# Normalizing one head of each retention pair on ScalarE instead of VectorE, in a two-layer streaming encoder

## The chip, the cores and the metric

One core of one Trainium2 chip runs the whole program. The metric is the device time of one execution in microseconds; lower is better. A core has five engines that run their own instruction streams in order and wait for each other through semaphores: TensorE (PE, with its weight loads as PEld), VectorE (DVE), ScalarE (ACT), GpSimd (POOL) and SyncE (SP), whose queue starts the DMA transfers. L12 in a profile line is line 12 of the kernel.

## What is computed

A sequence of 1024 tokens with 1024 channels passes through two layers. The first holds a state-space mixer and, beside it, a retention with 8 heads. Only the end of the retention is touched here:

```python
out = (intra_out + cross).reshape(bsz, seq, RET_HEADS, RET_DV)     # 8 heads of 128
mu = jnp.mean(out, axis=-1, keepdims=True)
var = jnp.mean(jnp.square(out - mu), axis=-1, keepdims=True)
out = (out - mu) * lax.rsqrt(var + EPS)
...
y_ret = retention(q, k, v).astype(h.dtype) * jax.nn.silu(g_ret)
```

Each token's 128 values of a head are centred and divided by their spread. The result is multiplied by a gate and goes, with the state-space branch, through an output projection; then come the convolution layer and a last norm.

## The kernel before

Nearly all large products are written as three TensorE matmuls of a high and a low part of each operand (lines L277, L278, L279), so TensorE has work through the whole program. The other engines prepare operands: a weight tile `wf` is loaded by DMA, ScalarE casts it to its high part `wh`, and VectorE or GpSimd makes the low part `wl`.

The retention runs over four pairs of heads (`ret_heads`, once for each pair). Within a pair the 1024 tokens are two halves `hf` of four blocks `b4` of 128 tokens; `hh` is the head within the pair. For one half and one head:

- TensorE makes the 128x512 result `ro` in PSUM, one 128x128 block for each `b4`.
- VectorE takes statistics of each block (`st` at L1246, `mv` with mean and variance at L1247).
- ScalarE takes the square root into `rs` (L563), VectorE the reciprocal in place (L564).
- VectorE writes `on` = (block - mean) * `rs`, four instructions (L1252).
- TensorE transposes `on` into `rt` (L1260), and VectorE multiplies `rt` with the gate into `grl` (L1263).

Both heads' transposes of the first half stand on TensorE ahead of both heads' of the second half, with the head `hh` = 1 first each time, in one fixed chain of order. The tile `on` has three buffers, so the fourth `on` of a pair (second half, `hh` = 1) takes the buffer of the pair's first one and can be written only after that one's transposes.

Around this, TensorE works on the gated linear unit of the state-space branch (`mm_glu`), 24 matmuls for a block and half. ScalarE applies a tanh to each result in place (L1094, or L1325 in the later blocks) and VectorE multiplies it into `yg` (L1095), which SyncE stores. A further background chain, `weight_low`, loads half weight tiles `lf`, casts them on ScalarE into `lh` (L233), makes the low part on GpSimd or VectorE (L234) and stores it, for the second layer. After the transposes of a pair come the next pair's `ktp` transposes, VectorE's `kt` (L1170), and TensorE's `kv` products (L1187), which need `kt`.

A scheduler sets the order of each engine's instructions when the program is built, by priorities and its own estimate of times. The engines then keep that order, so an instruction that waits holds up everything behind it on its engine. Square roots and tanh need different tables on ScalarE; ACT_TABLE_LOAD rows mark a change of table.

Of the kernel before, what the change touches and what calls it, by code (L numbers as in the profile page):

```python
# [11 lines left out]
F32 = mybir.dt.float32  # L12
F32R = mybir.dt.float32r
I32 = mybir.dt.int32
AF = mybir.ActivationFunctionType
ALU = mybir.AluOpType
# [3 lines left out]
P = 128  # L20
# [39 lines left out]
class Trunk:  # L60
# [1098 lines left out]
    def ret_heads(self, pair, K, Q, qadds, V, turned):  # L1159
        nc, rp = self.nc, self.rp  # L1160
        v = nc.vector

        kt = rp.tile([P, 8, P], F32, name=f"kt_{pair}", tag="kt", bufs=1)
        for hf in range(2):
            ps = self.bank(f"ktp{hf}_{pair}")
            for b in range(4):
                t0 = (4 * hf + b) * P
                nc.tensor.transpose(ps[:, b * P:(b + 1) * P], K[:, t0:t0 + P], self.ident[:])
            kd = self.kdec[:, 2 * pair:2 * pair + 2, :].rearrange("p h d -> p (h d)")
            self.last_kt = v.tensor_tensor(kt[:, 4 * hf:4 * hf + 4, :], ps[:].rearrange("p (b d) -> p b d", b=4),  # L1170
                                           kd.unsqueeze(1).broadcast_to([P, 4, P]), op=ALU.mult)

        with self.tc.issue_after(self.last_kt.ins):
            for add in qadds:
                add()
        turned()

        S = rp.tile([P, 8, P], F32, name=f"S_{pair}", tag="S", bufs=1)
        for hf in range(2):
            ps = self.bank(f"kv{hf}_{pair}")  # L1180
            for b4 in range(4):
                b = 4 * hf + b4
                if b == 7:
                    continue
                for hh in range(2):
                    r = slice(64 * hh, 64 * hh + 64)
                    nc.tensor.matmul(ps[r, b4 * P:(b4 + 1) * P], kt[:, b, r], V(pair, b, hh),  # L1187
                                     start=True, stop=True)
            for b4 in range(4):
                b = 4 * hf + b4  # L1190
                if b == 7:
                    continue
                kv = ps[:, b4 * P:(b4 + 1) * P]
                if b == 0:
                    v.tensor_copy(S[:, 1, :], kv)
                else:
                    v.scalar_tensor_tensor(S[:, b + 1, :], S[:, b, :], self.g128[:, pair:pair + 1], kv,
                                           op0=ALU.mult, op1=ALU.add)

        self.masked = [None, None]  # L1200
        sc = [rp.tile([P, 8, P], F32, name=f"sc{hh}_{pair}", tag=f"sc{hh}", bufs=1) for hh in range(2)]
        for hf in range(2):
            sps = [self.bank(f"sp{hf}{hh}_{pair}") for hh in range(2)]
            self.chained(nc.tensor.matmul(sps[hh][:, b4 * P:(b4 + 1) * P],
                                          K[64 * hh:64 * hh + 64, (4 * hf + b4) * P:(4 * hf + b4 + 1) * P],
                                          Q[64 * hh:64 * hh + 64, (4 * hf + b4) * P:(4 * hf + b4 + 1) * P],
                                          start=True, stop=True)
                         for b4 in range(4) for hh in range(2))
            for hh in range(2):
                self.masked[hf] = v.tensor_tensor(  # L1210
                    sc[hh][:, 4 * hf:4 * hf + 4, :], sps[hh][:].rearrange("p (b i) -> p b i", b=4),
                    self.mask[:, 2 * pair + hh, :].unsqueeze(1).broadcast_to([P, 4, P]), op=ALU.mult)


        gts = []
        for hh in range(2):
            h = 2 * pair + hh
            gt = rp.tile([P, T], F32, name=f"grl_{h}", tag="grl", bufs=3)
            with self.tc.issue_after(self.masked[0].ins):
                nc.sync.dma_start(gt[:], self.gr_d[h * P:(h + 1) * P])  # L1220
            gts.append(gt)
        todo = []
        for hf in range(2):
            pss = [self.bank(f"ro{hf}_{2 * pair + hh}") for hh in range(2)]

            def products():
                for b4 in range(4):
                    b = 4 * hf + b4
                    for hh in range(2):
                        r = slice(64 * hh, 64 * hh + 64)  # L1230
                        if b:
                            yield nc.tensor.matmul(pss[hh][:, b4 * P:(b4 + 1) * P], Q[r, b * P:(b + 1) * P],
                                                   S[r, b, :], start=b4 == (hf == 0), stop=False)
                for hh in range(2):
                    for b4 in range(4):
                        b = 4 * hf + b4
                        yield nc.tensor.matmul(pss[hh][:, b4 * P:(b4 + 1) * P], sc[hh][:, b, :],
                                               V(pair, b, hh), start=False, stop=b4 == 3)
            last_ro = self.chained(products())
            ons = []  # L1240
            for hh in range(2):
                h, ps = 2 * pair + hh, pss[hh]
                st6 = rp.tile([P, 4, 6], F32, name=f"st_{h}_{hf}", tag="bst", bufs=2)
                mv = rp.tile([P, 4, 2], F32, name=f"mv_{h}_{hf}", tag="bmv", bufs=2)
                for b4 in range(4):
                    v.bn_stats(st6[:, b4, :], ps[:, b4 * P:(b4 + 1) * P])  # L1246
                    v.bn_aggr(mv[:, b4, :], st6[:, b4, :])  # L1247
                rs = rp.tile([P, 4], F32, name=f"rs_{h}_{hf}", tag="brs", bufs=2)
                self.last_rs = self.rsqrt(rs[:], mv[:, :, 1], eps=self.reps[:, h:h + 1])
                on = rp.tile([P, 4, P], F32, name=f"on_{h}_{hf}", tag="on", bufs=3)  # L1250
                for b4 in range(4):
                    v.tensor_scalar(on[:, b4, :], ps[:, b4 * P:(b4 + 1) * P], mv[:, b4, 0:1],  # L1252
                                                   rs[:, b4:b4 + 1], op0=ALU.subtract, op1=ALU.mult)
                ons.append(on)
            todo.append(ons)

            for hb in ((), (0, 1))[hf]:
                for hh in (1, 0):
                    tp = self.bank(f"rt{hb}_{2 * pair + hh}")
                    last_ro = self.chained((nc.tensor.transpose(tp[:, b4 * P:(b4 + 1) * P], todo[hb][hh][:, b4, :],  # L1260
                                                                self.ident[:]) for b4 in (3, 2, 1, 0)), last_ro)
                    c = slice(hb * HALF, (hb + 1) * HALF)
                    v.tensor_tensor(gts[hh][:, c], tp[:], gts[hh][:, c], op=ALU.mult)  # L1263
        for hh in range(2):
            h = 2 * pair + hh
            nc.sync.dma_start(self.yr_d[h * P:(h + 1) * P], gts[hh][:])
# [579 lines left out]
```

## Time and profile before

| | |
|---|---|
| time, 3 runs | 1177.71, 1180.71 (median), 1185.98 us |
| profiled execution, its own time | 1179.18 us |
| profiled execution, span of the trace | 1177.4 us |
| busy: PE, DVE, ACT, POOL | 1155.9, 954.2, 566.6, 718.3 us |
| granted TensorE clock, mean | 0.997 |
| retention pairs in the trace | about 517 to 635 us |

The span is what the instruction trace covers; the profiled execution's own time is 1.8 us longer. A timeline row gives the start, the length, the engine, the line, the operation with its output and inputs, how many equal instructions were merged, and in brackets how long the engine had been idle and what ended the wait. A window row gives for each engine the busy time and number of instructions in a stretch, and then the TensorE clock, the busy share of the DMA engines and their rate.

### The profile page before, as it was taken

Reading aid. Unit: us, or ns where it says so; the run is one execution under the profiler, and the core shown is the slowest. Engines: PE = TensorE matmul, PEld = TensorE weight load, DVE = VectorE, ACT = ScalarE, POOL = GpSimd, SP = SyncE. Lnnn points to the kernel's source line nnn. Section 1 sums busy time; section 2 is a strip of 40 time slices with the busy share of each in tenths; the row PEclk is TensorE's granted clock in tenths of the full one; section 3 lists DMA queues with packets and bytes.
Section 4 is the critical chain, followed back from the end, with each engine's and each line's share of the span. In section 5 each row is a group of like instructions: output and inputs, shape, how many; then the busy total and the mean of one; then the engine's idle time right before and its main releaser. Section 6 shows DMA issues by size and latency. Waiting matters only on the chain.

```text
span 1177.4 us, 17601 instructions
## 1 busy us (share of the span) xinstructions
PE 1155.9 (98%) x6102; PEld 958.2 (81%) x6102; DVE 954.2 (81%) x1541; ACT 566.6 (48%) x855; POOL 718.3 (61%) x499
## 2 busy tenths in 40 slices
PE   9999999999999999998999999999999999999997
PEld 7888788788887888877888788888888888888877
DVE  6889989999725666676888999579999999999643
ACT  7212342332236756413224846467756578544662
POOL 2049999888841143686532053439894689977742
PEclk9999999999999999999999999999999999999999
DMA  9359579877799979997676879975448653366863
GB/s 342 109 166 326 193 271 320 269 272 273 249 308 334 366 249 313 361 300 255 209 237 238 308 249 305 344 255 187 161 161 297 221 181 133 126 192 232 277 250 139
DMA packets 142137, 293.74 MB, mean 249 GB/s; under 512 B 14048, under 2 KB 42976, under 8 KB 141920
## 3 DMA queue, kind: packets, MB, share of 16 engines
q1 hardware_dynamic: 140896, 288.43, 72.2%
q10 hardware_dynamic: 1152, 4.19, 0.9%
q8 instruction: 48, 0.79, 0.3%
q14 instruction: 41, 0.34, 0.1%
HBM read 210.32 MB, written 81.20 MB: 248 GB/s over the span
## 4 chain that ended last, share of the span: by engine, by line
PE 70%; DVE 12%; DMA 10%; issue 3%; ACT 2%; SPq 1%; POOL 1%; DVEq 0%; ACTq 0%; POOLq 0%
PE mm_g L279 5%; PE mm_g L278 5%; PE mm_g L277 5%; PE mm_w L279 4%; PE mm_w L278 4%; PE mm_w L277 4%; PE mm_k L1026 4%; PE mm_a L279 2%; PE mm_b L278 2%; PE mm_a L278 2%; PE mm_b L279 2%; PE mm_a L277 2%; PE mm_b L277 2%; PE mm_oc L279 2%; PE mm_oc L278 2%
## 5 line engine op out<-in xcount | busy, mean ns | idle before, releaser
L1533 DVE SCALAR_TENSOR_TENSOR cv<-u,convw,cv 128x512 f32<-128x512 f32 x358 | 244.5, 748 | 4.5 <-ACT cv L1519 3.0
L1513 POOL TENSOR_TENSOR tp<-tp,tp 128x512 f32<-128x512 f32 x104 | 138.9, 1338 | 28.8 <-ACT tp L1512 23.5
L279 PE MATMUL mm_g<-xh,wl_g 128*128 128x512 f32 x256 | 100.8, 394 | 0.0
L278 PE MATMUL mm_g<-xl,wh_g 128*128 128x512 f32 x256 | 100.6, 393 | 0.0
L277 PE MATMUL mm_g<-xh,wh_g 128*128 128x512 f32 x256 | 100.4, 392 | 0.0
L1512 ACT ACTIVATE tp<-u,convw 128x512 f32<-128x512 f32 x104 | 69.8, 714 | 11.3 <-POOL tp L1513 11.0
L167 POOL TENSOR_TENSOR wl_K<-wf_K,wh_K 128x1024 fp32r<-128x1024 f32 x14 | 34.0, 2430 | 48.6 <-ACT wh_K L166 46.6
L278 PEld LDWEIGHTS mm_g<-xl,wh_g 128*128 128x128 f32 x256 | 48.1, 188 | 11.3 <-issue 1.6
L279 PEld LDWEIGHTS mm_g<-xh,wl_g 128*128 128x128 f32 x256 | 48.0, 188 | 10.5
L277 PEld LDWEIGHTS mm_g<-xh,wh_g 128*128 128x128 f32 x256 | 48.1, 188 | 9.6
L279 PE MATMUL mm_oc<-zh,wl_woc 128*128 128x512 f32 (+1 forms) x152 | 54.4, 359 | 0.6 <-DMA wl_woc<-lo_woc 0.6
L277 PE MATMUL mm_oc<-zh,wh_woc 128*128 128x512 f32 (+1 forms) x152 | 54.3, 361 | 0.0
L278 PE MATMUL mm_oc<-zl,wh_woc 128*128 128x512 f32 (+1 forms) x152 | 54.0, 356 | 0.0
L277 PE MATMUL mm_glu<-yh,wh_glu 128*128 128x512 f32 x128 | 51.2, 400 | 2.2 <-ACT yh L1270 2.2
L278 PE MATMUL mm_u<-xl,wh_u 128*128 128x512 f32 x128 | 50.0, 391 | 1.0 <-DVE xl L399 1.0
L278 PE MATMUL mm_glu<-yl,wh_glu 128*128 128x512 f32 x128 | 50.5, 394 | 0.2 <-DVE yl L1272 0.2
L279 PE MATMUL mm_glu<-yh,wl_glu 128*128 128x512 f32 x128 | 50.6, 396 | 0.0
L277 PE MATMUL mm_g<-h1h,wh_cg 128*128 128x512 f32 x128 | 50.3, 393 | 0.0
L277 PE MATMUL mm_a<-h1h,wh_ca 128*128 128x512 f32 x128 | 50.2, 392 | 0.0
L279 PE MATMUL mm_b<-h1h,wl_cb 128*128 128x512 f32 x128 | 50.2, 392 | 0.0
L279 PE MATMUL mm_a<-h1h,wl_ca 128*128 128x512 f32 x128 | 50.0, 390 | 0.0
L279 PE MATMUL mm_g<-h1h,wl_cg 128*128 128x512 f32 x128 | 49.8, 389 | 0.0
(834 smaller groups left out, 3671.9 us busy)
## 6 DMA issues: line engine op xcount, KB each, us to landing
wf_g<-w_ab SPq DMA_DIRECT2D x16, 512.0 KB, 6.2
a<-w_out SPq DMA_DIRECT2D x32, 256.0 KB, 4.5
ws<-a SPq DMA_DIRECT2D x32, 256.0 KB, 4.5
lf<-w_c SPq DMA_DIRECT2D x32, 256.0 KB, 5.1
wf_p<-ws SPq DMA_DIRECT2D x16, 512.0 KB, 4.8
wf_cb<-w_c SPq DMA_DIRECT2D x16, 512.0 KB, 5.0
wf_ca<-w_c SPq DMA_DIRECT2D x16, 512.0 KB, 4.8
wl_cb<-lo_cb SPq DMA_DIRECT2D x16, 512.0 KB, 3.3
```

What stands on the lines that cost most here:

```text
L167: e.tensor_tensor(wl[:].rearrange(fl), wf[:], wh[:].rearrange(fl).bitcast(F32), op=ALU.subtract)
L277: nc.tensor.matmul(ps, wh[:, kb, :], xh, start=start, stop=False, skip_group_check=chain)
L278: nc.tensor.matmul(ps, wh[:, kb, :], xl, start=False, stop=False, skip_group_check=chain)
L279: self.last_mm = nc.tensor.matmul(ps, wl[:, kb, :], xh, start=False, stop=stop, skip_group_check=chain)
L1026: self.last_mm = self.nc.tensor.matmul(ps, l[:, k, :], r[:], start=start and k == m == 0, stop=stop and k == 3 and m == 2, skip_group_chec ...
L1512: nc.scalar.mul(sk[:], u[:, k:k + HALF], cw[:, nb, k:k + 1])
L1513: gp.tensor_tensor(s0[:], s0[:], sk[:], op=ALU.add)
L1533: v.scalar_tensor_tensor(dst[:], *tap, accs_[i][:], op0=ALU.mult, op1=ALU.add)
```

## The change

For the head `hh` = 1 of each pair, the four VectorE instructions that made `on` become four ScalarE instructions `Identity(value * rs + nb)`. Their bias `nb` = -mean * `rs` is made for all four blocks by one VectorE instruction on a 128x4 tile. The head `hh` = 0 stays as it was.

```diff
                 on = rp.tile([P, 4, P], F32, name=f"on_{h}_{hf}", tag="on", bufs=3)
+                if hh:
+                    nb = rp.tile([P, 4], F32, name=f"nb_{h}_{hf}", tag="bnb", bufs=2)
+                    v.scalar_tensor_tensor(nb[:], mv[:, :, 0], -1.0, rs[:], op0=ALU.mult, op1=ALU.mult)
                 for b4 in range(4):
-                    v.tensor_scalar(on[:, b4, :], ps[:, b4 * P:(b4 + 1) * P], mv[:, b4, 0:1],
-                                                   rs[:, b4:b4 + 1], op0=ALU.subtract, op1=ALU.mult)
+                    o, p = on[:, b4, :], ps[:, b4 * P:(b4 + 1) * P]
+                    if hh:
+                        nc.scalar.activation(o, p, AF.Identity, scale=rs[:, b4:b4 + 1], bias=nb[:, b4:b4 + 1])
+                    else:
+                        v.tensor_scalar(o, p, mv[:, b4, 0:1], rs[:, b4:b4 + 1], op0=ALU.subtract, op1=ALU.mult)
                 ons.append(on)
```

Over the program 32 instructions move from VectorE to ScalarE and 8 small ones are added on VectorE. The new lines shift what follows by six: L1260 becomes L1266, L1263 becomes L1269. The scheduler then orders the engines anew. In the names below the first digit behind `rs`, `mv`, `nb` and `on` is the half of the tokens, behind `ro` and `rt` the head, behind `mm_glu` and `yg` the half; the last number tells buffers apart.

ScalarE in the first pair, from the second square root on. Before:

```order
L563 ACTIVATE rs_0_5132<-mv_0_5123,reteps 128x4
L563 ACTIVATE rs_1_5168<-mv_1_5159,reteps 128x4
L563 ACTIVATE rs_1_5186<-mv_1_5177,reteps 128x4
L233 CAST lh_5297<-lf_5296 128x512
L268 CAST wh_glu_5532<-wf_glu_5531 128x1024
L1094 ACT_TABLE_LOAD
L1094 ACTIVATE mm_glu_1_5264<-mm_glu_1_5264,hgb 128x512
L1094 ACTIVATE mm_glu_0_5542<-mm_glu_0_5542,hgb 128x512
L233 CAST lh_5303<-lf_5302 128x512
```

And with the change:

```order
L563 ACTIVATE rs_0_5132<-mv_0_5123,reteps 128x4
L1257 ACTIVATE on_0_5135<-ro_1_5089,nb_0_5136,rs_0_5132 128x128 x4
L563 ACTIVATE rs_1_5170<-mv_1_5161,reteps 128x4
L563 ACTIVATE rs_1_5188<-mv_1_5179,reteps 128x4
L233 CAST lh_5301<-lf_5300 128x512
L268 CAST wh_glu_5540<-wf_glu_5539 128x1024
L1094 ACT_TABLE_LOAD
L1094 ACTIVATE mm_glu_1_5268<-mm_glu_1_5268,hgb 128x512
L1257 ACTIVATE on_1_5191<-ro_1_5143,nb_1_5192,rs_1_5188 128x128 x4
L233 CAST lh_5307<-lf_5306 128x512
L1094 ACTIVATE mm_glu_0_5550<-mm_glu_0_5550,hgb 128x512
```

The second half's four `on` now stand behind the first tanh, and the next cast `lh` has moved from behind the second tanh to ahead of it.

VectorE at the same place, from the reciprocals of the second half on. Before:

```order
L564 RECIPROCAL rs_1_5168<-rs_1_5168 128x4
L1252 TENSOR_SCALAR on_1_5171<-ro_0_5140,mv_1_5159,rs_1_5168 128x128 x4
L564 RECIPROCAL rs_1_5186<-rs_1_5186 128x4
L1095 SCALAR_TENSOR_TENSOR yg_1_5259<-mm_glu_1_5264,yg_1_5259 128x512
L1252 TENSOR_SCALAR on_1_5189<-ro_1_5141,mv_1_5177,rs_1_5186 128x128 x4
L1263 TENSOR_TENSOR grl_5086<-rt_1_5194,grl_5086 128x512
```

And with the change:

```order
L564 RECIPROCAL rs_1_5170<-rs_1_5170 128x4
L1259 TENSOR_SCALAR on_1_5173<-ro_0_5142,mv_1_5161,rs_1_5170 128x128 x4
L564 RECIPROCAL rs_1_5188<-rs_1_5188 128x4
L1253 SCALAR_TENSOR_TENSOR nb_1_5192<-mv_1_5179,rs_1_5188 128x4
L1095 SCALAR_TENSOR_TENSOR yg_1_5263<-mm_glu_1_5268,yg_1_5263 128x512
L1269 TENSOR_TENSOR grl_5086<-rt_1_5198,grl_5086 128x512
```

The bias stands ahead of the multiplication that waits for the tanh, where the four `on` had stood behind it.

TensorE at the first half's transposes of the first pair, with the change:

```order
L279 MATMUL mm_glu_0_5550<-yh_0_4615,wl_glu_4909 128x512
L277 MATMUL mm_glu_0_5550<-yh_0_4621,wh_glu_4908 128x512
L1266 MATMUL rt_1_5198<-ident,on_0_5135 128x128 x4
L1266 MATMUL rt_0_5204<-ident,on_0_5117 128x128 x4
L278 MATMUL mm_glu_0_5550<-yl_0_4622,wh_glu_4908 128x512
```

The second row stood behind the transposes before: one matmul more now comes ahead of them. TensorE's order is otherwise the same but for seven other single matmuls that moved by a few places. In the later projection stage ScalarE's seven last `lh` casts (`lh` 25 to 31) stand one to seven places earlier among its casts of `wh` and operands. On ScalarE two table loads of the last pair are gone.

## The prediction

> **What bounds the kernel now.** I read the page first, then a table of windows over the retention pairs, then TensorE's waits in that stretch.
>
> ```profile
> span 1177.4 us, 17601 instructions
> PE 1155.9 (98%) x6102; PEld 958.2 (81%) x6102; DVE 954.2 (81%) x1541; ACT 566.6 (48%) x855; POOL 718.3 (61%) x499
> 525.00:555.00 30.00, 26.72 (x185) 22.38 (x184) 20.65 (x70) 10.56 (x15) 23.31 (x17) 1.00 0.78 248
> 555.00:580.00 25.00, 25.00 (x171) 21.45 (x169) 20.54 (x70) 7.42 (x10) 13.75 (x12) 1.00 0.78 243
> 580.00:605.00 25.00, 23.55 (x191) 19.90 (x189) 21.61 (x72) 7.90 (x11) 9.60 (x6) 1.00 0.54 169
> 605.00:635.00 30.00, 29.21 (x212) 25.11 (x213) 25.21 (x80) 8.48 (x12) 9.30 (x7) 1.00 0.76 265
> 635.00:660.00 25.00, 25.00 (x110) 20.02 (x109) 21.77 (x32) 13.00 (x22) 2.00 (x2) 1.00 0.90 324
> PE rt L1260 <- DVE mv L1247: 2.4, 1, 2.4
> PE rt L1260 <- DVE on L1252: 2.1, 2, 1.2
> ```
>
> TensorE is busy for 1155.9 of 1177.4 us, so the whole program has 21.5 us to win without taking work from TensorE, and the change takes none. In a window row the first figure behind the width is TensorE's busy time: in the 110 us of the four pairs it is idle for 3.28 + 0 + 1.45 + 0.79 = 5.5 us. That is the most the change can win here. The last two rows (waiter, releaser, total us, times, longest) name most of it, transposes that wait for the normalization; one wait of `kv` for `kt` comes below. VectorE is busy for 88.0 of the 110 us, ScalarE for 34.4; neither is a bound by its sum. So only four places count, and at each the question is when the last input arrives. Behind the stage (last window) TensorE is full; what is won or lost before passes on to the end.
>
> **What one instruction costs.**
>
> ```profile
> L563 ACT ACT_TABLE_LOAD x11 | 14.1, 1283 | 0.2
> L563 ACT ACTIVATE rs<-mv,reteps 128x4 f32<-128x4 f32 x16 | 4.6, 297 | 40.0 <-DVE mv L1247 40.0
> L1252 DVE TENSOR_SCALAR on<-ro,mv,rs 128x128 f32<-128x128 f32 x64 | 21.7, 402 | 0.3
> L1595 DVE SCALAR_TENSOR_TENSOR cn<-cst,cn 128x4 f32<-128x4 f32 x2 | 0.3, 156 | 2.9 <-ACT cn L1594 2.9
> L830 ACT ACTIVATE R<-s_s_m,s_r 128x128 f32<-128x128 f32 x32 | 10.1, 391 | 25.1 <-DVE v L874 12.7 <-POOL s_bbr L618 12.5
> L1512 ACT ACTIVATE tp<-u,convw 128x512 f32<-128x512 f32 x104 | 69.8, 714 | 11.3 <-POOL tp L1513 11.0
> L1508 ACT ACTIVATE tp<-u,vecs,convw 128x512 f32<-128x512 f32 x16 | 13.1, 816 | 5.3 <-POOL tp L1513 3.1 <-DVE u L1475 1.7 <-issue 0.2
> L1128 ACT ACTIVATE v<-mm_v,Rtok 128x512 f32<-128x512 f32 x8 | 5.0, 696 | 0.6 <-PE mm_v L1110 0.6
> ```
>
> The new ScalarE instruction is not in the trace. The nearest row is L830: same size, a scale for each partition, no bias, 391 ns. L1508 is L1512 with a bias tile: 816 - 714 = 102 ns more. L1128 reads PSUM where L1512 reads SBUF: 18 ns less. So one takes about 0.475 us. L830's busy time is 10.1/32 = 0.316 us for one, so neighbours overlap by 0.075: four take 0.475 + 3 x 0.40 = **1.67 us**, against 1.36 on VectorE. From both sides: without any price for the bias 1.36, with no overlap 1.90. The bias tile is the same kind of instruction as L1595: 0.16 us.
>
> VectorE loses 32 x 21.7/64 = 10.8 us and gains 8 x 0.16 = 1.2, so it is relieved by 9.6 us. ScalarE takes 8 x 1.67 = 13.4 us more, and 2 x 1.28 less for the two table loads that go. These sums cost and bring nothing by themselves, as long as each engine is hidden behind TensorE.
>
> The Trainium skill (ScalarE: Activation LUTs, Rules for kernel authors) tells the author to put plain multiplies and adds on VectorE, not on ScalarE. The rows agree for a single instruction, 475 against 402 ns. By that rule alone all eight groups would each lose 0.31 us, 2.5 us in all, and the time would be 1181.7; the sum below counts the loss only where TensorE waits for it.
>
> **Pair 0, the four places in order.**
>
> ```profile
> 536.28 1.35 DVE L1252 TENSOR_SCALAR on<-ro,mv,rs 128x128 f32<-128x128 f32 x4
> 541.17 0.17 DVE L564 RECIPROCAL rs<-rs 128x4 f32<-128x4 f32 x1
> 543.44 0.69 DVE L1095 SCALAR_TENSOR_TENSOR yg<-mm_glu,yg 128x512 f32<-128x512 f32 x1 [2.10 <-POOL lh L234]
> 544.05 1.36 DVE L1252 TENSOR_SCALAR on<-ro,mv,rs 128x128 f32<-128x128 f32 x4
> 547.12 1.27 DVE L1263 TENSOR_TENSOR grl<-rt,grl 128x512 f32<-128x512 f32 x2
> 542.68 1.24 ACT L1094 ACTIVATE mm_glu<-mm_glu,hgb 128x512 f32<-128x512 f32 x2
> 547.99 0.62 ACT L233 CAST lh<-lf 128x512 fp32r<-128x512 f32 x1 [4.07 <-DMA lf<-w_c]
> 545.06 0.39 SPq L232 DMA_DIRECT2D lf<-w_c  x1
> 537.78 1.06 PE L1260 MATMUL rt<-ident,on 128*128 128x128 f32 x8 [2.37 <-DVE mv L1247]
> 545.46 1.09 PE L1260 MATMUL rt<-ident,on 128*128 128x128 f32 x8 [0.91 <-DVE on L1252]
> 552.38 1.75 PE L1187 MATMUL kv<-v,kt 128*64 128x128 f32 x28
> ```
>
> *First transposes (537.78).* They start 0.15 us after `on` ends at 537.63. Now VectorE starts the bias at 536.28, where `on` had started; ScalarE begins at 536.46 and ends at 538.13, and the transposes start at 538.28: 0.50 late. One `mm_glu` matmul now comes ahead of them; at 25.00/110 = 0.227 us it fits into the wait. Net **+0.27**.
>
> *Second transposes (545.46).* Before, their `on` stood behind the `yg` multiplication, which had waited for the tanh (ended about 543.30); it ended at 545.41. Now the bias is ready soon after 541.34 and ScalarE goes on right behind the tanh: 543.32 to 544.99. Transposes at 545.04, **-0.42** against before, and this includes the +0.27. If VectorE's relief also brings the tanh forward, the bound is TensorE itself, which arrives at 545.46 - 0.91 + 0.27 = 544.82: at best -0.64.
>
> *`kv` (552.38).* Here the order adds a wait. The cast `lh` now stands ahead of the second tanh. Its load was issued at 545.06 and the cast began at 547.99. The issue stays where it is, because SyncE first stores the `yg` that follows the first tanh. So the second tanh moves from 543.3 to 548.5 and ends at 549.15. Queued behind it is VectorE's `yg`, and behind that two `grl` and `kt`: 549.15 + 0.65 + 1.2 + 0.65 (a `kt` has the size of a `grl`) puts the end of the first `kt` at 551.65. `kv` now wants it at 552.38 - 0.42 = 551.96. It fits, with 0.3 us to spare: **0**, and all of the 0.42 passes on.
>
> **Pairs 1, 2 and 3.**
>
> ```profile
> 566.53 1.35 DVE L1252 TENSOR_SCALAR on<-ro,mv,rs 128x128 f32<-128x128 f32 x4
> 570.54 1.03 PE L1260 MATMUL rt<-ident,on 128*128 128x128 f32 x8
> 576.91 1.03 PE L1260 MATMUL rt<-ident,on 128*128 128x128 f32 x8
> 601.38 1.37 DVE L1252 TENSOR_SCALAR on<-ro,mv,rs 128x128 f32<-128x128 f32 x4
> 602.66 2.47 DVE L1263 TENSOR_TENSOR grl<-rt,grl 128x512 f32<-128x512 f32 x4
> 602.80 1.09 PE L1260 MATMUL rt<-ident,on 128*128 128x128 f32 x8 [1.22 <-DVE on L1252]
> 605.79 1.42 PE L1187 MATMUL kv<-v,kt 128*64 128x128 f32 x22 [1.02 <-DVE kt L1170]
> ```
>
> In pair 1 no transpose waits. The first `on` ends at 568.4 instead of 567.9, 2.1 us before use. The second is now behind a table load, a tanh, another table load and the square root: from 568.4, + 0.30 + 1.28 + 0.62 + 1.28 + 0.30 + 0.17 + 0.16 + 1.67 = 574.2, still 2.7 us ahead of 576.91. Pair 3 has no wait either. Both **0**, covered by `mm_glu` matmuls; without that cover each first transpose would cost 0.5 us.
>
> In pair 2 the second `on` takes the buffer that the first transposes still read, so it can't start before 601.38 on ScalarE either. It ends at 603.05, and the second transposes start 0.30 us later. VectorE, though, has done the first two of its four `grl` by then; the other two and `kt` follow the transposes, and `kt` comes about when it did. `kv` sets the end of this place: **0**, between -0.4 (VectorE's relief reaches `kt`) and +0.3.
>
> **The sum.** 1179.18 (the profiled execution's own time) - 0.42 = **1178.8 us**. The median of the three runs is 1180.71, 1.5 above that execution, so on the scale of medians the same sum gives 1180.3. I take the middle, **1179.5**; the likeliest case's own range is 1177 to 1182.
>
> **Rivals.**
>
> ```profile
> DMA to landing us min/median/max: 2.9/5.5/7.5
> 507.50:510.00 2.50, 1.34 (x4) 0.85 (x4) 1.36 (x1) 1.18 (x2) 2.50 (x2) 0.74 0.76 256
> 510.00:512.50 2.50, 2.28 (x10) 1.86 (x10) 0.97 (x3) 1.32 (x2) 2.50 (x2) 0.58 0.96 266
> 542.50:545.00 2.50, 2.06 (x10) 1.36 (x8) 1.56 (x4) 1.41 (x3) 2.50 (x3) 1.00 0.11 42
> ACT lh L233 <- DMA lf<-w_c: 9.6, 6, 3.1
> ```
>
> *A, ScalarE's queue becomes the new wait (slower).* The first row is the time to landing of the twelve `lf` loads between 500 and 760 us. The one ahead of the second tanh in pair 0 took 2.9, the shortest. It costs once it takes over 3.2 us, and at 3.6 the gain is gone. With the median of 5.5 `kv` waits 2.3 us: 1178.8 + 2.3 = 1181.1. With 7.5 it waits 4.3, and a long wait can take clock too: after the stall at 507 us the granted clock was 0.74 and 0.58 for 2.5 us each, (0.26 + 0.42) x 2.5 = 1.7 us. That gives 1184.8. For it: the median. Against: the load meets nearly idle DMA engines (share 0.11 just before), and the order of SyncE ahead of it is unchanged. Chance 0.20. The Trainium skill (TensorE: Matmul & The Clock Gate, Why this matters for your kernels) asks for no idle gap over about 3 us; by that 2.3 us would keep the clock and 4.3 lose it. In this trace an idle of 2.37 us at 537.78 kept it at 1.00.
>
> *B, VectorE's relief clears every wait (faster).* Each wait of TensorE in the stage names VectorE, which gets 9.6 us back. Then all 5.5 us go: 1173.7. Against it: `on` comes no sooner from ScalarE, as worked out. Chance 0.12.
>
> *C, the projections pay (slower).* The seven `lh` casts that moved ahead there wait for loads too (last row: 9.6 us in six waits, longest 3.1). A wait of 3.1 us ahead of a weight's cast that TensorE needs gives 1181.9. Against: those waits stood ahead of such casts before as well, and TensorE was full in the window 635 to 660. Chance 0.10.
>
> The forecast keeps 0.58.
>
> **How the numbers follow.** The range runs from 1174.5, near all of B, to 1186, A's worst with 1.2 us for the distance of medians. Within 1% of before, 11.8 us, is about what a measurement of this kernel can't tell from no change. All 5.5 us of B are half of that, and A's worst is 5.6 above 1179.18. So faster by over 1% gets 0.02, slower 0.06 (A or C at several places, with the clock lost each time), and 0.92 lies between.
>
> **What would show it.** Right: ScalarE's `on` near 0.47 us; the first transposes of pair 0 about 0.5 us later behind `on`, the second with no or half the wait; `lh` idle for its load ahead of a tanh, and `kv` of pair 1 without a wait; VectorE's busy time lower by about 10 us with TensorE's unchanged. Wrong: `kv` waiting for `kt` by over 1 us there (A), TensorE idle for under 2 us in the four pairs (B), or new waits for `wl` behind 640 us (C).

## The result and the profile after

The changed kernel takes **1184.53 us** at the median (1178.87 to 1191.72, 22 runs) against 1180.62 us for the kernel before in the same comparison (1176.82 to 1185.98, 22 runs): ratio **1.0035**, 95% interval 1.0022 to 1.0049. That is 3.9 us slower, within the predicted range but on the other side from the forecast of 1179.5 us. Two later comparisons gave 1.0060 (1.0040 to 1.0081) and 1.0034 (1.0012 to 1.0057). The ratio is not the quotient of the two medians; where they differ, the ratio and its interval decide. One execution each of two later kernels took 1911 and 5572 us and is left out of the ratios.

The changed kernel's page, the two rows that answer to those of before:

```profile
span 1184.0 us, 17612 instructions
PE 1157.4 (98%) x6102; PEld 957.5 (81%) x6102; DVE 947.7 (80%) x1517; ACT 574.6 (49%) x885; POOL 722.2 (61%) x499
```

Its windows (width, then busy time of TensorE, its weight loads, VectorE, ScalarE and GpSimd, then granted clock, DMA share, GB/s), the last one new:

```profile
525.00:555.00 30.00, 25.43 (x142) 21.31 (x144) 18.13 (x59) 13.15 (x23) 22.14 (x17) 0.89 0.77 250
555.00:580.00 25.00, 25.00 (x192) 21.46 (x187) 17.93 (x62) 10.36 (x19) 16.10 (x12) 1.00 0.66 217
580.00:605.00 25.00, 23.56 (x189) 19.97 (x187) 19.91 (x68) 6.31 (x15) 7.99 (x6) 1.00 0.64 173
605.00:635.00 30.00, 29.09 (x219) 24.86 (x220) 23.84 (x72) 12.69 (x23) 6.61 (x5) 1.00 0.72 246
635.00:660.00 25.00, 23.33 (x99) 17.87 (x98) 20.22 (x29) 11.66 (x19) 3.98 (x3) 1.00 0.86 304
735.00:750.00 15.00, 12.34 (x53) 9.52 (x52) 15.00 (x13) 8.88 (x14) 10.23 (x7) 1.00 1.03 378
```

That last window in before:

```profile
735.00:750.00 15.00, 15.00 (x67) 12.24 (x66) 11.62 (x10) 6.42 (x10) 12.05 (x8) 1.00 1.00 341
```

And the changed kernel's waits of TensorE (waiter, releaser, total us, times, longest):

```profile
PE rt L1266 <- ACT on L1257: 6.3, 2, 4.6
PE mm_w L279 <- DVE wl_p L167: 2.7, 2, 2.1
PE mm_w L277 <- ACT ysh L1303: 1.5, 2, 1.0
PE kv L1187 <- DVE kt L1170: 0.7, 1, 0.7
```

In the four pairs TensorE is now idle for 4.57 + 0 + 1.44 + 0.91 = 6.9 us instead of 5.5, and the clock of the first window is 0.89. Behind the pairs TensorE was full in before; now it is idle for 1.67 us in 635 to 660 (`mm_w` waits for `ysh`) and for 2.66 us in 735 to 750 (`mm_w` waits for `wl_p`). This execution took 1185.78 us, 6.6 more than the profiled one of before; 3.9 is the difference of medians.

**Where the first pair loses.** The changed kernel's timeline there (start, duration, engine, in brackets the idle time ahead and its releaser), with one bias of the second pair at the end:

```profile
536.31 1.06 DVE L1253 SCALAR_TENSOR_TENSOR nb<-mv,rs 128x4 f32<-128x4 f32 x1
536.09 2.48 POOL L1004 TENSOR_TENSOR kraw<-kraw,ropek 128x512 f32<-128x512 f32 x2
537.40 1.50 ACT L1257 ACTIVATE on<-ro,nb,rs 128x128 f32<-128x128 f32 x4 [2.88 <-DVE nb L1253]
538.96 1.97 PE L1266 MATMUL rt<-ident,on 128*128 128x128 f32 x8 [4.57 <-ACT on L1257]
569.03 0.15 DVE L1253 SCALAR_TENSOR_TENSOR nb<-mv,rs 128x4 f32<-128x4 f32 x1
```

And the answer on the bias's line, with the shortest, median and longest of its eight durations in ns:

```profile
L1253 DVE SCALAR_TENSOR_TENSOR nb<-mv,rs x8: 140/1000/1284, 536.3 to 630.4; 128x4 f32<-128x4 f32 x8
```

The prediction gave the bias 0.16 us. It takes that only where GpSimd is idle, as at 569.03; the median is 1.00 us. At 536.31 it ends at 537.37, where the first of GpSimd's two products ends (536.09 + 2.48/2 = 537.33). The Trainium skill (SBUF — State Buffer, SBUF: two separate sides) says that a VectorE instruction with two inputs in SBUF and a GpSimd instruction that reads SBUF take the same port pair, and that whichever starts first keeps the other out for its whole length. The bias has two such inputs, `mv` and `rs`; the `tensor_scalar` that it helps to replace reads its tile from PSUM. The trace agrees here: short with GpSimd idle, long and ending with GpSimd's product otherwise. By that page the change had a rival that the prediction lacked.

**Where the projection loses.** The changed kernel's timeline: GpSimd's sum `u`, SyncE's load, VectorE, TensorE.

```profile
717.66 5.93 POOL L1414 TENSOR_TENSOR u<-u,xr 128x512 f32<-128x512 f32 x1 [7.61 <-DMA xr<-xT]
724.51 1.41 SPq L1342 DMA_DIRECT2D yr1f<-yr_d  x1
721.75 0.68 DVE L1422 TENSOR_TENSOR yr1f<-yr1f,t2f 128x512 f32<-128x512 f32 x1
729.33 0.69 DVE L1422 TENSOR_TENSOR yr1f<-yr1f,t2f 128x512 f32<-128x512 f32 x1 [6.90 <-DMA yr1f<-yr_d]
739.83 0.50 PE L279 MATMUL mm_w<-t40h,wl_p 128*128 128x512 f32 x1 [2.15 <-DVE wl_p L167]
```

SyncE's longest wait in it between 700 and 735 us (waiter, releaser, total, times, longest):

```profile
SPq L1415 <- POOL u L1414: 6.7, 1, 6.7
```

The same sum in before:

```profile
714.06 1.74 POOL L1408 TENSOR_TENSOR u<-u,xr 128x512 f32<-128x512 f32 x1 [7.88 <-DMA xr<-xT]
```

The sum for `u2_1` takes 5.93 us instead of 1.74. SyncE's next transfer is the store of that sum, and SyncE waits 6.7 us for it. Behind it in the same queue stands the load of `yr1f7`, issued at 724.51. VectorE is idle for 6.90 us ahead of the instruction that needs that load and then busy without a break (15.00 of 15.00 us in the window 735 to 750); `wl_p` stands in that row, and TensorE waits. In before the load stands behind the same store too, and the two were issued at 716.25 and 715.83: new is the length of the sum, not the order of these two. Nothing of this stretch is in the diff: the scheduler moved casts, loads and VectorE's subtractions there.

### The profile page after: what moved, and what is told of

It is laid out like the page before. It is cut to its first block, busy times and chain, and to the rows that moved or that the text cites. A ratio compares the mean times of both kernels' runs of the same rounds, so it can differ in the third digit from the quotient of the medians.

```text
span 1184.0 us, 17612 instructions
## 1 busy us (share of the span) xinstructions
PE 1157.4 (98%) x6102; PEld 957.5 (81%) x6102; DVE 947.7 (80%) x1517; ACT 574.6 (49%) x885; POOL 722.2 (61%) x499
## 4 chain that ended last, share of the span: by engine, by line
PE 70%; DMA 13%; DVE 10%; issue 2%; ACT 2%; POOL 2%; SPq 1%; DVEq 0%; ACTq 0%; POOLq 0%
PE mm_g L279 7%; PE mm_g L278 7%; PE mm_g L277 7%; PE mm_a L279 2%; PE mm_a L278 2%; PE mm_b L278 2%; PE mm_a L277 2%; PE mm_b L277 2%; PE mm_b L279 2%; PE mm_oc L279 2%; PE mm_oc L278 2%; PE mm_oc L277 2%; DMA lf<-w_c 2%; PE mm_k L1026 2%; PE mm_v L1109 2%
## 5 line engine op out<-in xcount | busy, mean ns | idle before, releaser
L277 PE MATMUL mm_u<-xh,wh_u 128*128 128x512 f32 x128 | 49.5, 397 | 0.5 <-ACT wh_u L268 0.4
```

What stands on the lines that cost most here:

```text
L277: nc.tensor.matmul(ps, wh[:, kb, :], xh, start=start, stop=False, skip_group_check=chain)
```

## The experiments

Three theories. **1:** the bias waits for GpSimd, and what is late behind it is the loss. **2:** the tiles stand in ScalarE's queue. **3:** the other order of the projection costs. The times of one kernel scatter by 2 to 4 us (standard deviation), so a comparison of 12 runs with some 30 of before resolves about 1.7 us; waits in one trace tell the place, the medians the size. In each table: median of this kernel, median of before in the same comparison, ratio and its 95% interval.

### The bias column by column

```diff
-v.scalar_tensor_tensor(nb[:], mv[:, :, 0], -1.0, rs[:], op0=ALU.mult, op1=ALU.mult)
+for b4 in range(4):
+    v.tensor_scalar(nb[:, b4:b4 + 1], mv[:, b4, 0:1], rs[:, b4:b4 + 1], -1.0, op0=ALU.mult, op1=ALU.mult)
```

> The bias is made by four tensor_scalar instructions of 128x1, each with one tensor from SBUF (the mean) and the factor as a per-partition scalar, in place of one instruction with two tensors from SBUF; ScalarE normalizes as in the changed kernel; from the output projection on, the order on every engine is that of the kernel before. Theory 1 (the bias instruction waits for GpSimd's running instruction, and what is late behind it is the loss): no bias instruction over 0.3 us, the four together under 0.6 us, the wait of TensorE for the first pair's normalized tiles near 2.9 us instead of 4.57, and the time within 1 us of before. Theory 2 (the queue of ScalarE: the tiles are late because they stand in its queue): 3 to 4 us over before, like the change. Theory 3 (the other order of the projection's casts costs): within 1 us of before, but with the first pair's wait still near 4.6 us.

| | us | before | ratio |
|---|---|---|---|
| bias by column | 1182.05 | 1178.64 | 1.0016 (0.9997 to 1.0035) |

The 32 instructions take 194 to 215 ns each, a group of four 0.56 us, and none waits for GpSimd. The order behind the pairs is that of before and there is no wait for `wl_p`; the first pair's wait is 0.51 us where 2.9 was expected. Yet the kernel is 0.16% over before (3.4 us by the medians, where 1 was expected). Its profile has a wait of 2.61 us at the third pair's transposes (before: 1.22), behind which the granted clock was 0.71 and 0.61 for 2.5 us each, and one of 0.77 for `ysh`. That does not fit theory 1 alone, and the interval, which takes in no difference, is too wide to say more.

### The move in some pairs only

```diff
-if hh:
+if hh and pair == 0:        # in the other two: pair in (1, 2), pair == 3; both places
```

> Only the first pair of heads is normalized on ScalarE; the other three as before; the projection's order is that of before. Theory 1: the two bias instructions take 1.0 to 1.2 us, TensorE waits 4 to 4.6 us for the first transposes and loses some clock behind it: 1 to 2.5 us over before. Theory 2: about 1 us over. Theory 3: within 0.5 us of before.

> Only the second and third pair are normalized on ScalarE; the queue of SyncE and the order on GpSimd are exactly those of before. Theory 1: bias instructions of up to 1.3 us again, but only the third pair's transposes wait for them, 1.7 us and 0.7 us on the next: 0 to 0.7 us over before. Theory 2: 0.5 to 1.5 us over. Theory 3: within 0.3 us.

> Only the last pair is normalized on ScalarE; from there on the order on every engine is that of the changed kernel, casts of the projection included. Theory 1: the second bias instruction takes 1.3 us, the last tanh comes 2 us late or more, and TensorE waits for its operand at the start of the output projection: 1 to 2.5 us over before, with no wait for wl_p that before does not have. Theory 2: 1 to 2 us over. Theory 3: 3 to 4.5 us over, with waits for wl_p of 2 to 3 us near 735.

| ScalarE normalizes in | us | before | ratio |
|---|---|---|---|
| first pair | 1181.20 | 1178.64 | 1.0017 (0.9998 to 1.0035) |
| second and third | 1178.82 | 1178.64 | 0.9993 (0.9973 to 1.0014) |
| last pair | 1182.22 | 1178.64 | 1.0017 (0.9993 to 1.0042) |

The middle pairs show no cost. The last pair, moved alone, brings the whole chain of the projection with it: GpSimd's sum takes 6.97 us and TensorE waits 3.2 us for `wl_p`. That wait is what theory 3 expected and theory 1 did not; the time, 0.17% over before, can't be told from it. The first pair's wait was 2.09 us, not the 4 to 4.6 of theory 1, though its biases took 1.11 and 1.22 us; its profile loses elsewhere. VectorE, GpSimd and TensorE at the third pair in that kernel:

```profile
590.27 3.03 DVE L1014 TENSOR_TENSOR krot<-kraw,kswp 128x512 f32<-128x512 f32 x2
589.81 2.94 POOL L1004 TENSOR_TENSOR qraw<-qraw,ropek 128x512 f32<-128x512 f32 x2 [12.30 <-DVE sc L1210]
603.59 1.09 PE L1266 MATMUL rt<-ident,on 128*128 128x128 f32 x8 [2.96 <-DVE on L1259]
```

VectorE's same row in before:

```profile
591.22 1.28 DVE L1014 TENSOR_TENSOR krot<-kraw,kswp 128x512 f32<-128x512 f32 x2
```

GpSimd's `qraw`, which in before started at 594.24, here meets VectorE's `krot`, both with SBUF operands: 3.03 us instead of 1.28, and the transposes wait 1.7 us longer (2.96 against 1.22); behind that wait the clock was 0.72 and 0.60 for 2.5 us each. It is the same meeting of the two engines, at a place that the edit doesn't touch.

### The bias with one input from PSUM, the store behind the load, and both

With one input from PSUM the bias takes four columns of the product in place of the means, so this kernel leaves out the right bias.

```diff
-v.scalar_tensor_tensor(nb[:], mv[:, :, 0], -1.0, rs[:], op0=ALU.mult, op1=ALU.mult)
+v.scalar_tensor_tensor(nb[:], ps[:, 0:4], -1.0, rs[:], op0=ALU.mult, op1=ALU.mult)
```

```diff
-nc.sync.dma_start(self.ux_d[rows(r)], z[:])
+with self.tc.issue_after(self.yr1f_dma.ins) if r == 1 else nullcontext():
+    nc.sync.dma_start(self.ux_d[rows(r)], z[:])
```

> The changed kernel once more, as the base for the three runs beside it. All theories: 3 to 5 us over before, bias instructions of about 1.1 us at the first pair, a wait for wl_p of 2 to 3 us near 735 to 740.

> The bias instruction takes the first four columns of the product's PSUM bank in place of the means, so that only one of its two tensors lies in SBUF; what is left out is the right bias, everything else and the order on every engine is that of the changed kernel. Theory 1 (the bias instruction waits for GpSimd's running instruction because both of its tensors lie in SBUF): every bias instruction under 0.25 us, the first transposes of the first pair 0.9 us earlier behind the same factor, 1 to 2.5 us under the changed kernel. Theory 2 (ScalarE's queue): the bias may be short, but the time stays within 0.7 us of the changed kernel. If the bias instruction waits for GpSimd for another reason than its operands, it stays at 1 us and the time at that of the changed kernel.

> The changed kernel with one difference on one queue: on SyncE the store of u2_1 stands four places later, behind the load of yr1f7. Theory 3 (the other order of the projection costs, by this chain: GpSimd's sum u2_1 is drawn out by VectorE, the store waits for it, the load behind the store comes late, VectorE waits 7 us for it and wl_p is late): the load is issued near 716 instead of 724, VectorE's wait of 7 us goes, TensorE waits under 0.6 us for wl_p, and the time is 2 to 4 us under the changed kernel. Theory 1 alone and theory 2: within 0.7 us of the changed kernel.

> Both edits together: the bias with one of its tensors from PSUM (the right bias is left out) and the store of u2_1 behind the load. Theories 1 and 3 together: both stalls gone, -0.5 to +1.5 us against before, so 3 to 5 us under the changed kernel. Theory 2: 2 us or more over before still, because ScalarE does the same work in the same order.

| | us | before | ratio |
|---|---|---|---|
| changed kernel (6 runs) | 1185.91 | 1179.53 | 1.0060 (1.0040 to 1.0081) |
| bias from PSUM | 1182.05 | 1179.53 | 1.0022 (1.0005 to 1.0038) |
| store behind the load | 1182.53 | 1179.53 | 1.0030 (1.0010 to 1.0049) |
| both | 1180.06 | 1179.53 | 1.0014 (0.9999 to 1.0028) |

The changed kernel, run again, showed both stalls: 6.86 us for the sum, 0.87 and 1.58 us of TensorE's waits for `wl_p` near 740. The bias from PSUM, the answer on its line:

```profile
L1253 DVE SCALAR_TENSOR_TENSOR nb<-ro,rs x8: 139/146/163, 533.4 to 625.7; 128x4 f32<-128x4 f32 x8
```

and its timeline at the first pair (the factor, the bias, ScalarE, TensorE):

```profile
532.57 0.17 DVE L564 RECIPROCAL rs<-rs 128x4 f32<-128x4 f32 x1
533.43 0.14 DVE L1253 SCALAR_TENSOR_TENSOR nb<-ro,rs 128x4 f32<-128x4 f32 x1
533.61 1.51 ACT L1257 ACTIVATE on<-ro,nb,rs 128x128 f32<-128x128 f32 x4 [1.97 <-DVE nb L1253]
535.17 1.09 PE L1266 MATMUL rt<-ident,on 128*128 128x128 f32 x8 [0.97 <-ACT on L1257]
```

All eight biases are short, none over 0.163 us, with the order of every engine unchanged: where the second input lies decides whether the bias waits. From the factor to the transposes it is 2.60 us here (535.17 - 532.57), 3.51 in the changed kernel (538.96 - 535.45, its factor's start), 2.36 in before (537.78 - 535.42). So the long bias costs the first pair 0.91 us and the move without it 0.24. The other traces agree wherever the factors stand as here: 3.51 to 3.73 us with a long bias, 2.59 or 2.60 with a short one, 2.36 where the first pair is that of before. TensorE's wait itself says less, since it also depends on when TensorE comes: with the first pair of before it was 2.37, 1.72, 3.11 and 0.75 us in four traces. Theory 1's mechanism is shown; its share of the time is not sharp (below).

The store alone missed its purpose. SyncE's next transfer, the load of `xr5_1`, waits for the same sum, since it reuses the buffer that the sum reads: SyncE waited 6.2 us there, `yr1f7` was issued at 720.15, and VectorE waited 6.69 us as before. So the store was the wrong thing to move. By the medians the kernel is still 3.4 us under the six runs of the changed kernel beside it, as was expected, but with both stalls in its profile: nothing shown here explains that, and those six runs are a weak base. In the kernel with both edits the sum happened to take 1.72 us, and no wait for `wl_p` came: with the sum short, the rest of the chain goes.

### The sum on VectorE, alone and with the other edits

```diff
-gp.tensor_tensor(z[:], z[:], x_tile(r, 1)[:], op=ALU.add)
+(v if r == 1 else gp).tensor_tensor(z[:], z[:], x_tile(r, 1)[:], op=ALU.add)
```

> The changed kernel with the sum u2_1 (128x512, two tensors from SBUF) on VectorE instead of GpSimd; the heads are those of the changed kernel. Theory 3 with its chain (VectorE's unbroken row of instructions with two tensors from SBUF keeps GpSimd's sum waiting for 6 us, and SyncE's queue stands behind it): the sum takes 0.7 us, SyncE is not held for 6 us, VectorE waits under 2.5 us for yr1f, TensorE under 0.6 us for wl_p, and the time is 2 to 3.5 us under the changed kernel, 1.5 to 3.5 us over before. Theory 1 alone and theory 2: within 0.7 us of the changed kernel.

> Once more the changed kernel with the sum u2_1 on VectorE, beside its partners on one chip. Theory 1 (the bias instruction's wait) with theory 3 (the late load): 0 to 2 us over before, 2.5 to 4.5 us under the changed kernel. If theory 3 is the whole: within 0.7 us of before.

> The same with the bias instruction's first tensor from PSUM, which leaves out the right bias; the order is the same on every engine. Theory 1: every bias instruction under 0.25 us, and 0.7 to 2 us under e7_again. If the bias instruction's wait is covered by the other waits of the heads: within 0.7 us of it.

> The kernel before with the sum u2_1 on VectorE. In before that sum takes 1.7 us on GpSimd and no load waits long behind it, so by theory 3 nothing is gained: within 0.7 us of before. If the sum on VectorE is a gain of its own: 1 us or more under before.

> The changed kernel, as the base on the same chip: 3 to 6 us over before; GpSimd's sum u2_1 takes 5 us or more, and TensorE waits 2 us or more for wl_p.

| | us | before | ratio |
|---|---|---|---|
| changed, sum on VectorE | 1180.08 | 1178.48 | 0.9994 (0.9972 to 1.0015) |
| the same again | 1180.93 | 1179.03 | 1.0019 (1.0000 to 1.0037) |
| and the bias from PSUM | 1179.57 | 1179.03 | 1.0007 (0.9986 to 1.0029) |
| before, sum on VectorE | 1179.73 | 1179.03 | 1.0008 (0.9989 to 1.0028) |
| changed kernel | 1183.24 | 1179.03 | 1.0034 (1.0012 to 1.0057) |

The timeline of that kernel in its second run (the sum, the load of `yr1f7`, the last two of VectorE's instructions that use such loads):

```profile
716.15 0.68 DVE L1414 TENSOR_TENSOR u<-u,xr 128x512 f32<-128x512 f32 x1
716.55 0.43 SPq L1342 DMA_DIRECT2D yr1f<-yr_d  x1
720.30 0.68 DVE L1422 TENSOR_TENSOR yr1f<-yr1f,t2f 128x512 f32<-128x512 f32 x1
722.52 0.68 DVE L1422 TENSOR_TENSOR yr1f<-yr1f,t2f 128x512 f32<-128x512 f32 x1
```

One instruction on another engine, and the late load, VectorE's wait of 6.9 us and TensorE's wait for `wl_p` are gone. Within this comparison the ratio falls from 1.0034 to 1.0019 (0.15%, 1.8 us), and within that of the next section from 1.0038 to 1.0005 (0.33%, 3.9 us). With the bias short the same chain shows less: 1.0022 with it (bias from PSUM), 1.0014 without (both edits), 0.08% or 1 us. So the late load and what hangs on it is worth 1 to 4 us by single comparisons. Over all of them the changed kernel's mean ratio is 1.0043 and that with the sum on VectorE 1.0007. In before the same edit gains nothing, so it hides no loss of the heads.

What stays for the heads, bias and move together, is 0.07% in the mean of two comparisons (0.9994 and 1.0019), not told from zero. The bias from PSUM took 1.4 us from the median of this kernel. From the changed one beside it, it took 0.38% (1.0060, six runs, to 1.0022), but it is only 0.08% under the kernel with the store moved, which had both stalls too (1.0030). How much the bias's wait costs by itself, between nothing and some 4 us, stays open.

### The cast ahead of the first pair's factors

In before ScalarE's square roots of the first pair stand behind the cast `lh_21`, which waits for its load. The change moves that cast behind them:

```diff
-LOWS, K_LOWS, V_LOWS, H_LOWS = 24, 20, 6, (0, 2, 4, 4)
+LOWS, K_LOWS, V_LOWS, H_LOWS = 24, 20, 6, (0, 1, 3, 4)
```

> The kernel before with one number of a table changed, so that ScalarE's cast lh_21, which waits for a load, stands behind the factors of the first pair instead of ahead of them. If the wait of TensorE at the first pair's transposes (2.4 us in the profile of before) comes from that load: the factors are made near 530.5 instead of 533.6, TensorE waits under 0.6 us there, and the time is 2 to 4 us under before. If the statistics are what it waits for: no change of over 0.7 us.

> The changed kernel with the same number changed. Theory 1: the bias instructions of the first pair may still take 1 us, but its transposes have the 3 us that the earlier factors give, TensorE waits under 1 us for them, and the time is 2 to 4 us under the changed kernel; what is left over the kernel before with that number changed is the projection's 2 to 3.5 us. Theory 2: the difference to the kernel before with that number changed stays at 4 us or more.

> The changed kernel with both edits, the table's number and the sum u2_1 on VectorE. Theories 1 and 3: both stalls gone; 1 to 3 us under before, within 1 us of the kernel before with the table's number changed. Theory 2: 2 us or more over that one.

| table changed in | us | before | ratio |
|---|---|---|---|
| before | 1180.83 | 1178.48 | 1.0016 (0.9996 to 1.0035) |
| changed kernel | 1182.38 | 1178.48 | 1.0038 (1.0016 to 1.0059) |
| changed, sum on VectorE | 1178.98 | 1178.48 | 1.0005 (0.9986 to 1.0023) |

The wait at the first pair went as expected in all three: 0.33 us in the first, 0.18 in the second, none listed in the third. The time did not follow: no kernel is faster than before, and the expected gain of 2 to 4 us missed. In the first, part of it comes back at once:

```profile
544.23 4.26 DVE L1014 TENSOR_TENSOR qrot<-qraw,qswp 128x512 f32<-128x512 f32 x2
545.15 2.79 POOL L269 TENSOR_TENSOR wl_glu<-wf_glu,wh_glu 128x1024 fp32r<-128x1024 f32 x1
548.64 0.46 PE L1204 MATMUL sp<-qrot,krot 64*128 64x128 f32 x2 [1.59 <-DVE qrot L1014]
```

Behind the transposes TensorE now meets `qrot` held up by GpSimd: 4.26 us for two, where two `krot` of the same size took 1.28 in the row of before above. In the other two the third pair's transposes wait 2.41 us (before: 1.22), and behind that the clock was 0.50 and 0.72 for 2.5 us. Where the rest went is open. The last two rows of the table tell the late load once more: GpSimd's sum takes 6.38 us in the slower one, and it is 0.33% slower.

### All profiles by the length of GpSimd's sum

| order behind the pairs | sum `u2_1` on GpSimd, us | TensorE waits 2 us or more for `wl_p` |
|---|---|---|
| as before: before, bias by column, first pair, middle pairs, table in before | 1.74, 1.40, 1.54, 1.50, 1.60 | none |
| as in the change: three of the changed kernel, last pair, bias from PSUM, store behind, table in the change | 5.93, 6.86, 6.75, 6.97, 6.80, 6.10, 6.38 | all seven |
| as in the change, both edits | 1.72 | no |

The seven profiles of the middle row are those of five kernels, with a mean ratio of 1.0034 over seven comparisons. The eight comparisons of kernels that hold the change, whole or in part, with that sum short or on VectorE have 1.0008: 0.26%, some 3 us. Which of the moved instructions makes the sum wait is not shown: the same seven carry the whole new order.

## Why the prediction was wrong

*The sum.* It gave -0.42 us; the medians say +3.9. Some 3 us of that lie in the projection (1 to 4 by single comparisons), for which the prediction had 0; what is left for the pairs can't be told from zero, where it had a gain of 0.42.

*The failed step: the projection.* Rival C named the place and the sign (the projection pays, TensorE waits for `wl`, 1181.9) and gave it 0.10. It looked for a late cast ahead of a weight on ScalarE; what came was GpSimd's sum held up by VectorE, and a load behind a store in SyncE's queue. My argument against it, that the waits stood there before and TensorE was full in the window 635 to 660, tested the wrong window: the loss is at 735 to 745. (635 to 660 lost 1.67 us as well, but waits for `ysh` there, of 0.5 and 1.3 us, stay in the kernel with the sum on VectorE.) The rows that move there were in the order; I counted ScalarE's casts and did not follow VectorE, GpSimd and SyncE.

*The mis-sized term: the bias.* Priced 0.16 us from L1595, measured 0.14 to 1.28 with median 1.00. L1595 takes one of its two inputs from PSUM (`cst`), the bias both from SBUF: a row of the same operation and size was not the same kind of instruction. With the short bias the step stands: from factor to transposes 2.86 us by the prediction (538.28 - 535.42), 2.60 measured. The lower bound of 1.36 us for four `on` is not what its terms give: without the bias's 102 ns one is 0.373, and four are 0.373 + 3 x 0.298 = 1.27.

*Right.* Four `on` take 1.50 us, one 457 ns at the median (predicted 1.67 and 475). The second transposes of the first pair wait no longer. Rival A's chain ran and was covered, as forecast: the cast waits for its load with the tanh behind it, and `kv` does not wait. The rows of the changed kernel:

```profile
547.93 0.62 ACT L233 CAST lh<-lf 128x512 fp32r<-128x512 f32 x1 [3.38 <-DMA lf<-w_c]
548.46 0.65 ACT L1094 ACTIVATE mm_glu<-mm_glu,hgb 128x512 f32<-128x512 f32 x1
554.37 1.75 PE L1187 MATMUL kv<-v,kt 128*64 128x128 f32 x28
```

Pair 1 has no wait, pair 2 one of 1.68 and 0.67 us where 1.22 and 1.02 had been. VectorE's busy time fell by 6.5 us, not 9.6: the eight biases take 6.0 us together instead of 1.3.

*The clock.* The prediction let only rival A's longest wait take clock. It was taken at the first transposes, behind the wait of 4.57 us: 0.89 over the window 525 to 555, which no term of the sum held. The other two traces of the changed kernel lost it there too (waits of 3.31 and 4.51 us), one of them also behind the wait for `wl_p` (2.20 us); with the sum on VectorE the same heads waited 2.42 and 2.46 us and kept it. Over whole executions the granted clock is 0.995 to 0.9955 at the median of the changed kernel's runs in its three comparisons, and 0.9965 and 0.997 with the sum on VectorE; 0.001 to 0.002 of 1180 us is, as an estimate, 1 to 2 us. So part of the loss may be clock, and the runs don't separate what the first pair's stall and what the one at `wl_p` takes of it.

Theory 2 has no loss left that these runs can tell from zero: with both meetings of VectorE and GpSimd taken away and ScalarE doing the same work, the time can't be told from before (1.0007, 0.9986 to 1.0029).

## What to carry to other kernels

Before adding a small instruction on VectorE, look where its inputs lie and what GpSimd runs beside it: two SBUF inputs made a 0.14 us instruction last 1.00 us at the median here, one input from PSUM made it 0.15. When a scheduler reorders, follow the order past the edit to the end of the program, on the DMA queue too: a transfer that waits for a slow engine holds every load behind it. And taking away the stall that a profile shows at one place can be worth nothing until the next place is read: three kernels kept 0.33 us or less of the first pair's wait, and none was faster than before.

## What the runs showed of the hardware

**VectorE can keep GpSimd out for a whole row of instructions.** The end of that row in the changed kernel, three of its rows:

```profile
718.21 0.68 DVE L1278 TENSOR_TENSOR t12l<-yr1f,t12h 128x512 fp32r<-128x512 f32 x1
720.01 0.68 DVE L1278 TENSOR_TENSOR t15l<-yr1f,t15h 128x512 fp32r<-128x512 f32 x1
720.62 1.22 DVE L167 TENSOR_TENSOR wl_p<-wf_p,wh_p 128x1024 fp32r<-128x1024 f32 x1
```

GpSimd's sum begins at 717.66 by the trace. VectorE goes on without a gap and unslowed until 722.43; the sum ends at 723.59, 1.16 us later, about what one such sum takes by itself. In all seven traces with a long sum it ends 1.14 to 1.16 us behind VectorE's row. In before the same sum got in after one instruction, and there VectorE's `t12l` took 1.79 us instead of 0.68. The rule of the Trainium skill that the first to start keeps the other out for its whole length (SBUF — State Buffer, SBUF: two separate sides) fits both, but does not say why one side is passed over six times running (eight in another run of the same kernel). What decides it, the runs don't show.

**An idle of TensorE costs clock, but not from one length on.** A window behind the first transposes of the kernel with the bias from PSUM and the store moved, which had waited 2.86 us there:

```profile
537.50:540.00 2.50, 2.50 (x8) 1.98 (x8) 1.27 (x6) 2.47 (x3) 2.50 (x3) 0.54 0.50 178
```

The same window of the kernel with ScalarE in the middle pairs, after a wait of 3.11 us:

```profile
537.50:540.00 2.50, 2.50 (x12) 2.06 (x11) 1.48 (x6) 2.48 (x4) 2.50 (x3) 1.00 0.27 95
```

The shorter wait lost half the clock, the longer none. Over all traces the timelines list 23 waits of TensorE of 2 us or more between 520 and 740 us. Behind ten of them, of 2.20 to 4.57 us, the clock fell; behind thirteen, of 2.06 to 3.11 us, it didn't. All of 3.17 us and more lost it. Two stretches behind the wait of 3.17 us for `wl_p` in the kernel with only the last pair on ScalarE:

```profile
737.34:739.84 2.50, 2.50 (x6) 2.02 (x7) 2.50 (x3) 2.50 (x6) 2.47 (x2) 0.50 0.94 298
739.84:742.34 2.50, 2.50 (x7) 1.92 (x7) 2.50 (x3) 1.50 (x3) 0.88 (x1) 0.50 0.99 297
```

The stretch after these had 0.80, so this stall cost (0.50 + 0.50 + 0.20) x 2.5 = 3.0 us of full clock on top of its own length, by estimate; the smallest of the ten cost 1.7. So a price for clock behind a stall of 2 to 3 us is a chance, not a number.
